# RWKV-7 mixer: operands laid out for both directions or both heads at once, score products in column halves

## Chip, cores and metric

One core of one Trainium2 chip runs the whole program. The metric is device time in microseconds (us), the median of three runs. Beside it there is one profiled execution, from which every row below comes.

## What is computed

The reference is a two-layer trunk over 1024 latent tokens and 256 context tokens (width 1024). A layer mixes tokens with three groups of heads (RWKV-7 in both directions, windowed attention, neighbourhood attention), all fed by one input projection, and then runs a hierarchical mixture of experts. The change is in the RWKV-7 group alone: 4 heads of 64, two directions, 1280 steps each of

```python
def _rwkv7_step(state, inp):
    r, w, k, v, kk, a = inp
    sk = jnp.einsum('dbhvk,dbhk->dbhv', state, kk)
    state = state * w[..., None, :] - sk[..., :, None] * (kk * a)[..., None, :] + v[..., :, None] * k[..., None, :]
    return state, jnp.einsum('dbhvk,dbhk->dbhv', state, r)
```

## The kernel before

`layer` runs per layer: layer norm and the part of the input projection that RWKV needs, then `rwkv`, then attention, output projection, routing, experts. While `rwkv` runs, the rest of the input projection (`in_A_rest`, `in_BC`; matmuls of L528 to L530 and L539 to L541) is issued piece by piece through `more()`, so that the two share TensorE.

`rwkv` works in chunks of 64 tokens. One **stage** `st` of ten takes 128 tokens (2 chunks, index `c`) of the forward direction and 128 of the backward one (`d`), for 4 heads as 2 pairs (`hp`) of 2 (`e`). Head `e` of a pair lives on partitions 0 to 63 or 64 to 127 (`hom[e]`). The parts of a stage:

- `front(st)` (L719 to L790), one stage ahead: decays by a scan along tokens (L746, one instruction per direction and head pair), exponentials, then the operands. `L1` holds kk times decay and r times decay: eight products of 64x256, four on VectorE (`e`=0) and four on GpSimd (`e`=1), L776 and L777. `bk` holds b and k (L784 on VectorE, L785 on GpSimd), `bw` (L788, GpSimd) is `bk` times the chunk's decay.
- Transposes of `bw` into `L2` (L809, copies L812).
- **Scores**: for each direction, eight products `pa` of [b|k] with [kk|r], 128x128 (L824), in two PSUM tiles. From each, VectorE masks the other head's half into `L1` (L829), a quarter into `Ly` (L831), and for `d`=1 another quarter into `low` (L833). For `d`=0 `low` has its own product `pf` (L840, L841). `pu`, `pb`, `pa` and `pf` share a ring of two PSUM buffers.
- **Inverse**: `low` goes to DRAM and comes back as lanes; `inv16` inverts the 16x16 diagonal blocks with 28 small VectorE instructions (L955, L956), and the result comes back through DRAM (L960, L963). Then `mm8` (L853) does three rounds of 16 products 64x64x64 (`pe4`, `pzt`, `pz`), each followed by a VectorE operation of 128x512 (L857, L858, L859), and L864 to L878 do the last 32x32 step.
- **State**: two steps per stage (`s`). Each is `px` (L904), a copy to `xy` (L906), `pu2` (L912), a negation split over ScalarE and VectorE (L913, L914), `pm` for the next state and the output (L924, L926), the new state (L930), and `ys`, the output, in four VectorE additions of 64x128 (L935). The value rows of the next state tile come by four ScalarE copies of 64x256 (`new_pvu`, L713). `ys` is stored once per stage (L940, two DMAs); `values` loads v with two DMAs (L705).

The code gives the order only in part: a scheduler in the framework orders each engine's queue by its own estimates of readiness, and every engine runs its queue strictly in that order. SyncE (SP) issues all these DMAs from one queue, and waits in it.

Of the kernel before, what the change touches and what calls it, by code (L numbers as in the profile page):

```python
# [9 lines left out]
F32 = mybir.dt.float32  # L10
# [12 lines left out]
P = 128  # L23
# [132 lines left out]
def _consts():  # L156
# [33 lines left out]
    for k in range(2):  # L190
        d[f"mL1_{k}"] = np.concatenate([np.concatenate([im[k], sm[k]], 1), np.concatenate([sm[k], im[k]], 1)], 0)
        d[f"mR_{k}"] = np.concatenate([im[k], im[k]], 0)
# [3 lines left out]
    d["mE4"] = np.concatenate([e4, e4], 0)  # L196
    d["scan"] = np.tile((np.arange(128) % 64 != 0).astype(np.float32), (128, 1))
# [106 lines left out]
class Trunk:  # L304
# [370 lines left out]
    def rwkv(self, l, rp, ps, tag, psc, tagc, psi, rest, more):  # L675
# [23 lines left out]

        vt = {}  # L700

        def values(st):
            vt[st] = rp.tile([P, 2, 2, 2, 64], F32, tag="vt", name="vt", bufs=2)
            for d, seg in enumerate((FSEG[st], BSEG[st])):
                nc.sync.dma_start(vt[st][:, d], self.vst[:, 2 * seg:2 * seg + 2])  # L705


        def new_pvu(st, s):
            t = rp.tile([P, 2, 2, 2, 2, 64], F32, tag="pvu", name="pvu", bufs=2)
            for d in range(2):  # L710
                for e in range(2):
                    o = hom[1 - e]
                    a.copy(t[o, d, :, :, e, :], vt[st][o, d, s if d == 0 else 1 - s].unsqueeze(1).to_broadcast([64, 2, 2, 64]))  # L713
            return t
# [4 lines left out]
        def front(st):  # L719
# [51 lines left out]
            L1v = L1.rearrange("p d c h e s t -> p d h e s c t")  # L771
            bku = bk.rearrange("p d h c s t -> p (d h c) s t")
            for d in range(2):
                for e in range(2):
# [6 lines left out]

            for e in range(2):
                o = hom[e]
                v.scalar_tensor_tensor(bku[o, :, e], units(b2)[o], 0.5, units(wv)[o], OP.mult, OP.mult)  # L784
                g.tensor_tensor(bku[o, :, 1 - e], units(kd)[o], units(wv)[o], OP.mult)  # L785

# [6 lines left out]
        for st in range(10):  # L793
# [16 lines left out]
            for e, pb in enumerate(pbs):  # L810
                for d in range(2):
                    a.copy(L2[:, d, :, :, e].rearrange("p c h t -> p h c t"), pb[:, 256 * d:256 * d + 256].rearrange("p (h c t) -> p h c t", h=2, c=2))  # L812

            def mask(m, p, n):
                return k2(m)[p].unsqueeze(1).unsqueeze(1).to_broadcast([p.stop - p.start, 2, 2, n])

            for d in range(2):

                pas = [ps.tile([P, 512], F32, tag=tag, name="pa") for _ in range(2)]
                for hp in range(2):  # L820
                    for c in range(2):
                        i = 2 * hp + c
                        for e in range(2):
                            te.matmul(pas[e][:, i * 128:i * 128 + 128], bk[hom[e], d, hp, c].rearrange("p s t -> p (s t)"),  # L824
                                      L1[hom[e], d, c, hp, e].rearrange("p s t -> p (s t)"), start=True, stop=True)
                for e, pa in enumerate(pas):
                    home, oth = hom[e], hom[1 - e]
                    pav = pa.rearrange("p (h c s t) -> p h c s t", h=2, c=2, s=2)
                    v.tensor_tensor(L1[oth, d, :, :, e].rearrange("p c h s t -> p h c (s t)"), pav[oth].rearrange("p h c s t -> p h c (s t)"),  # L829
                                    mask(f"mL1_{d}", oth, 128), OP.mult)  # L830
                    v.tensor_tensor(Ly[home, d].rearrange("p c h t -> p h c t"), pav[home, :, :, 1 - e], mask(f"mR_{d}", home, 64), OP.mult)  # L831
                    if d == 1:
                        v.tensor_tensor(low[home, 1], pav[home, :, :, e], mask("mLow", home, 64), OP.mult)  # L833

            pf = ps.tile([P, 512], F32, tag=tag, name="pf")
            for hp in range(2):
                for c in range(2):
                    for e in range(2):
                        i = 2 * hp + c
                        te.matmul(pf[hom[e], i * 64:i * 64 + 64], L1[hom[e], 0, c, hp, e, e, :], bk[hom[e], 0, hp, c, e, :], start=True, stop=True)  # L840
            v.tensor_tensor(low[:, 0], pf[:, 0:256].rearrange("p (h c t) -> p h c t", h=2, c=2), mask("mLow", slice(0, 128), 64), OP.mult)  # L841
# [6 lines left out]

            def mm8(name, lt, rh):
                o = psi.tile([P, 512], F32, tag="i", name=name)  # L850
                for u in range(8):
                    for e in range(2):
                        te.matmul(o[hom[e], u * 64:u * 64 + 64], lt[hom[e], u, :], rh[hom[e], u, :], start=True, stop=True)  # L853
                return o.rearrange("p (u t) -> p u t", t=64)
# [1259 lines left out]
```

## Time and profile before

| | us |
|---|---|
| median of three runs (3547.73 to 3562.64) | 3548.71 |
| profiled execution | 3544.36 |
| its span on the core | 3541.6 |
| `rwkv` of the first layer, about | 240 to 720 |
| `rwkv` of the second layer, about | 2000 to 2480 |

| engine | busy us | share of the span |
|---|---|---|
| TensorE matmul (PE) | 2930.6 | 83% |
| VectorE (DVE) | 2285.5 | 65% |
| ScalarE (ACT) | 1544.1 | 44% |
| GpSimd (POOL) | 1007.7 | 28% |

Shares are averages over stages with different limits, so only the two stretches of `rwkv` count here. Waits are shown by the instruction that waited and by the one that released it. The profile leaves digits off the ends of names: `L` is `L1` or `L2`, `pu` also `pu2`, `c` a table of constants, `z` the tiles `z16` of the inverse.

### The profile page before, as it was taken

What the parts mean: (1) busy time and instruction counts of PE and PEld (TensorE: products, weight loads), DVE (VectorE), ACT (ScalarE), POOL (GpSimd) and SP (SyncE); (2) the same over time, 40 slices, a digit from 0 to 9 for tenths busy, and PEclk for the clock granted to TensorE, in tenths of its full rate; (3) what the DMA queues carried; (4) which work ended last, traced back from release to release, by engine and by line L of the source; (5) the groups of instructions that cost most, each with busy time, mean ns of one, the idle gap of its engine ahead of it and who ended that gap; (6) DMA issues with size and microseconds to landing.
All of it is one profiled execution on the core that took longest, in us unless ns stands there. A gap on an engine that the chain in (4) does not pass through costs nothing. (4 is left out here: it accounts for less than half of the span.)

```text
span 3541.6 us, 71217 instructions
## 1 busy us (share of the span) xinstructions
PE 2930.6 (83%) x28620; PEld 1833.0 (52%) x28620; DVE 2285.5 (65%) x4614; ACT 1544.1 (44%) x2769; POOL 1007.7 (28%) x998
## 2 busy tenths in 40 slices
PE   7998889989998788888737998898889866778864
PEld 4656567666755444443325565666666443334431
DVE  4356877368769454557678677783776845554775
ACT  4342444345643154456544434443565314343651
POOL 1122453134424211111165225331433321101113
PEclk9998889999999899999858988899899978888987
DMA  9764343282355789999862542433732769899995
GB/s 375 297 194 111 80 104 89 70 237 71 113 176 199 278 315 384 385 379 367 334 227 78 158 106 77 105 103 95 200 107 73 258 235 363 338 393 364 349 347 198
DMA packets 425468, 773.11 MB, mean 218 GB/s; under 512 B 211152, under 2 KB 340848, under 8 KB 394160
## 3 DMA queue, kind: packets, MB, share of 16 engines
q1 hardware_dynamic: 388048, 697.84, 56.7%
q0 software_dynamic: 36368, 68.07, 5.7%
q8 instruction: 227, 3.72, 0.4%
q10 hardware_dynamic: 720, 2.62, 0.3%
q14 instruction: 105, 0.86, 0.1%
HBM read 653.31 MB, written 114.97 MB: 217 GB/s over the span
## 5 line engine op out<-in xcount | busy, mean ns | idle before, releaser
L1664 PE MATMUL pgate<-wgp,hT 128*32 128x256 f16 (+2 forms) x1704 | 353.1, 376 | 101.8 <-ACT wgp L1613 60.8
L1664 PEld LDWEIGHTS <-hT 128*32 128x32 f16 (+2 forms) x3408 | 206.7, 108 | 334.0 <-issue 172.7
L529 PE MATMUL acc<-hL,wH 128*128 128x256 f16 (+2 forms) x1040 | 346.4, 334 | 13.4 <-POOL hL L486 13.4
L528 PE MATMUL acc<-hH,wH 128*128 128x256 f16 (+2 forms) x1040 | 345.6, 335 | 7.6 <-DVE hH L485 6.6
L530 PE MATMUL acc<-hH,wL 128*128 128x256 f16 (+2 forms) x1040 | 345.4, 333 | 0.0
L1704 PE MATMUL pd<-wdp,gT 128*32 128x256 f16 (+2 forms) x1704 | 221.1, 369 | 37.6 <-DVE gT L1691 21.6
L1195 POOL TENSOR_SCALAR s<-s,rd 128x640 f32<-128x640 f32 (+2 forms) x216 | 171.6, 794 | 222.3 <-DVE rd L1191 97.4
L1622 POOL DMA_INDIRECT xg<-hmoe,map x69 | 87.7, 1271 | 508.4 <-PE ptx L1628 454.5
L1664 PE MATMUL pgate<-wup,hT 128*32 128x256 f16 (+1 forms) x1224 | 196.9, 347 | 19.8 <-DVE wup L1614 12.7
L1614 DVE SCALAR_TENSOR_TENSOR wgp<-wg,wgp 128x2048 f16<-128x2048 f32 x74 | 166.4, 2287 | 63.2 <-ACT wgp L1613 63.1
L1614 DVE SCALAR_TENSOR_TENSOR wdp<-wd,wdp 128x2048 f16<-128x2048 f32 x74 | 166.5, 2287 | 46.9 <-ACT wdp L1613 46.9
L1184 ACT ACTIVATE s<-s,nm 128x640 f32<-128x640 f32 (+2 forms) x216 | 164.4, 763 | 66.1 <-DVE nm L1181 48.6
L1614 DVE SCALAR_TENSOR_TENSOR wup<-wu,wup 128x2048 f16<-128x2048 f32 x74 | 166.3, 2286 | 30.0 <-ACT wup L1613 27.7
L1208 PE MATMUL po<-pt,vt 128*64 128x128 f32 x1920 | 166.9, 288 | 20.2 <-DVE pt L1199 11.7
L1293 PE MATMUL acco<-wo,o 128*128 128x512 f16 x756 | 177.2, 388 | 0.0
L1704 PEld LDWEIGHTS <-gT 128*32 128x32 f16 (+2 forms) x1704 | 97.0, 108 | 147.4 <-DVE gT L1691 30.0
L1613 ACT ACTIVATE wdp<-wd 128x2048 f16<-128x2048 f32 x74 | 137.2, 1903 | 51.0 <-DMA wd<-w_down 44.1
L1717 POOL DMA_DIRECT2D ys<-y x66 | 51.7, 784 | 378.5 <-DVE y L1711 206.9
L1613 ACT ACTIVATE wup<-wu 128x2048 f16<-128x2048 f32 x74 | 137.3, 1903 | 48.7 <-DMA wu<-w_up 48.7
L1613 ACT ACTIVATE wgp<-wg 128x2048 f16<-128x2048 f32 x74 | 137.4, 1902 | 46.0 <-DMA wg<-w_gate 42.7
L1165 PE MATMUL pss<-k,qs 128*128 128x256 f16 (+1 forms) x552 | 127.5, 269 | 31.9 <-DVE mx L1178 18.4
L1672 ACT ACTIVATE sg<-pgate 64x512 f32<-64x512 f32 (+2 forms) x86 | 42.8, 498 | 251.9 <-PE pgate L1664 251.9
(420 smaller groups left out, 7424.2 us busy)
## 6 DMA issues: line engine op xcount, KB each, us to landing
wu<-w_up SPq DMA_DIRECT2D x64, 2048.0 KB
wd<-w_down SPq DMA_DIRECT2D x64, 2048.0 KB
wg<-w_gate SPq DMA_DIRECT2D x64, 2048.0 KB
wmod<-w_mod SPq DMA_DIRECT2D x48, 1024.0 KB
w<-w_in SPq DMA_DIRECT2D x41, 512.0 KB
ld<-ys SPq DMA_DIRECT2D x40, 384.0 KB
z<-inv SPq DMA_DIRECT2D x80, 128.0 KB
ys<-y POOLq DMA_DIRECT2D x20, 512.0 KB
```

Of the source, the lines that this page charges most:

```text
L528: self.nc.tensor.matmul(ov, H[:, k, :], hh, start=k == 0, stop=False)
L529: self.nc.tensor.matmul(ov, H[:, k, :], hl, start=False, stop=False)
L530: self.nc.tensor.matmul(ov, Lo[:, k, :], hh, start=False, stop=k == KD - 1)
L1165: te.matmul(pss[:, o:o + n], qs[:, e, Q], k1[:, e, k0:k0 + n], start=True, stop=False)
L1184: a.activation(s2[:, e, :nk], s2[:, e, :nk], AF.Exp, bias=nm[:, e:e + 1], scale=1.0 / SS, accum_out=den[:, e:e + 1])
L1195: g.tensor_scalar(s2[:, e, :nk], s2[:, e, :nk], rd[:, e:e + 1], SC_Q, OP.mult, OP.mult)
L1208: te.matmul(po[64 * e:64 * e + 64, 0:P], vt[:, kb, 64 * e:64 * e + 64], pt[:, e, x * P:x * P + P], start=x == 0, stop=x == len(kbs) - 1)
L1293: te.matmul(acc, o[:, zo, k] if k < KD - 1 else self.og_last[:, zo, tok], wo[:, zw, k, c], start=k == 0 and y == 0, stop=k == KD - 1 and y ...
L1613: nc.scalar.mul(t[:, 0, c], w[:, c], SC_W)
L1614: nc.vector.scalar_tensor_tensor(t[:, 1, c], w[:, c], SC_W, t[:, 0, c], OP.mult, OP.subtract)
L1664: te.matmul(p[off + i * m:off + i * m + m, :n], part(hT, zh)[:, k, o:o + m], part(w, zw)[:, k, i * n:i * n + n], start=k == 0 and y == 0, ...
L1704: te.matmul(t, part(gT, zh)[:, k, :m], part(wd, zw)[:, k, i * n:i * n + n], start=k == 0 and y == 0, stop=k == 3 and y == len(parts) - 1)
```

## The change

Tiles change their axis order so that one instruction covers both directions or both heads. Per stage:

- Scans: 2 of 128x256 in place of 4 of 128x128.
- `L1`: 4 products of 64x512, all on VectorE and placed behind `bk`, in place of 4+4 of 64x256 on VectorE and GpSimd.
- Scores: `pa` gives way to `pk` (16 products, 64 rows and 64 output partitions by 128 columns, one PSUM tile per direction), `pr` (16 of 64x64) for `Ly` and `pf` (16 of 64x64, 8 before) for `low`. Masks: four of 64x512 as before, and one 128x512 each for `Ly` and `low` in place of four, two and one of 256 columns.
- `mm8` computes only the 32 columns of each 64 that are used. Its three VectorE operations have 128x256.
- `L2` copies 2 for 4, value copies 2 for 4 per step, `ys` 1 addition of 128x256 for 4 of 64x128 per step.
- `ys` is stored per step, two DMAs of 64 KB; `values` takes three DMAs for two.

```diff
-                for hp in range(2):
-                    v.tensor_tensor_scan(cum[:, d, hp], k2("scan"), th[:, d, hp], 0.0, OP.mult, OP.add)
+                v.tensor_tensor_scan(cum[:, d].rearrange("p h t -> p (h t)"), k2("scan"), th[:, d].rearrange("p h t -> p (h t)"), 0.0, OP.mult, OP.add)
...
-                    eng = v if e == 0 else g
-                    eng.tensor_tensor(L1v[hom[e], d, :, e, e], chv(kk_)[hom[e], d], chv(ex)[hom[e], d], OP.mult)
-                    eng.tensor_tensor(L1v[hom[e], d, :, e, 1 - e], chv(r_)[hom[e], d], chv(cum)[hom[e], d], OP.mult)
...
+                for i, (x, y) in enumerate(((kk_, ex), (r_, cum))):
+                    v.tensor_tensor(L1p[o, :, :, e, i], pieces(x)[o], pieces(y)[o], OP.mult)
...
             for d in range(2):
-                pas = [ps.tile([P, 512], F32, tag=tag, name="pa") for _ in range(2)]
...
+                pk = ps.tile([P, 4, 128], F32, tag=tag, name="pk")
                 for hp in range(2):
                     for c in range(2):
                         for e in range(2):
+                            te.matmul(pk[hom[1 - e], 2 * hp + c], bk[hom[e], d, hp, c, 1 - e, :],
+                                      L1[hom[e], d, hp, c, e].rearrange("p s t -> p (s t)"), start=True, stop=True)
+                for e in range(2):
+                    o = hom[1 - e]
+                    v.tensor_tensor(L1[o, d, :, :, e].rearrange("p h c s t -> p (h c) (s t)"), pk[o],
+                                    k2(f"mL1_{d}")[o].unsqueeze(1).to_broadcast([64, 4, 128]), OP.mult)
+            pr = ps.tile([P, 8, 64], F32, tag=tag, name="pr")
+            pf = ps.tile([P, 8, 64], F32, tag=tag, name="pf")
...
+                            te.matmul(pr[hom[e], i], b_, r1, start=True, stop=True)
+                            x, y = (K_, b_) if d == 0 else (b_, K_)
+                            te.matmul(pf[hom[e], i], x, y, start=True, stop=True)
+            v.tensor_tensor(Ly.rearrange("p d h c t -> p d (h c) t"), pr.rearrange("p (d u) t -> p d u t", d=2),
...
+            v.tensor_tensor(low.rearrange("p d h c t -> p (d h c) t"), pf, k2("mLow").unsqueeze(1).to_broadcast([P, 8, 64]), OP.mult)
...
+                o = psi.tile([P, 8, 2, 16], F32, tag="i", name=name)
...
+                        te.matmul(o[hom[e], u], lt[hom[e], u, :], rh[hom[e], u], start=True, stop=True)
...
+            v.tensor_tensor(Eh, mm8("pe4", lowu, up16), k2("mE4").rearrange("p (g t) -> p g t", t=16).unsqueeze(1).to_broadcast([P, 8, 2, 16]), OP.mult)
+            pzt = mm8("pzt", z16, Eh)
+            v.tensor_tensor(up16, up16, pzt, OP.subtract)
+            v.tensor_tensor(lo16, lo16, mm8("pz", E4, lo16), OP.subtract)
...
+                ys = rp.tile([P, 2, 2, 64], F32, tag="ys", name="ys", bufs=2)
+                v.tensor_tensor(ys, pm[:, 1], xy[:, 1], OP.add)
+                for d in range(2):
+                    nc.sync.dma_start(y_d[d, 2 * seg[d] + cs[d]], ys[:, d])
```

The scheduler's order moves with it. On VectorE, late in the second layer's `rwkv`, from the last masks of one stage to the products of the next `front`, before (`c` is the table of masks, `pvu` the state tile):

```order
L829 TENSOR_TENSOR L_25074<-pa,c_20752 64x2x2x128
L831 TENSOR_TENSOR Ly<-pa,c_20752 64x2x2x64
L833 TENSOR_TENSOR low<-pa,c_20752 64x256
L930 TENSOR_TENSOR pvu<-pmy,xw 64x2x2x64 x2
L935 TENSOR_TENSOR ys<-pmy,xy 64x128 x4
L857 TENSOR_TENSOR E<-pe_25339,c_20752 128x512
L754 TENSOR_TENSOR cum<-ex,th 128x256
L761 SCALAR_TENSOR_TENSOR th<-ta,ld 128x512
L841 TENSOR_TENSOR low<-pf,c_20752 128x256
L784 SCALAR_TENSOR_TENSOR bk<-th,wv 64x8x64 x2
L776 TENSOR_TENSOR L_25642<-ld,ex 64x2x2x64 x2
L777 TENSOR_TENSOR L_25642<-ld,cum 64x2x2x64 x2
```

The same place with the change:

```order
L790 TENSOR_TENSOR L_25691<-ld,ex 64x8x64
L790 TENSOR_TENSOR L_25691<-ld,cum 64x8x64
L828 TENSOR_TENSOR L_25120<-pk,c_20784 64x4x128 x4
L923 TENSOR_SCALAR pvu<-pu_24930 64x4x64
L866 TENSOR_TENSOR E_20794<-pe_25396,c_20784 128x16x16
L938 TENSOR_TENSOR pvu<-pmy,xw 64x4x64 x2
L940 TENSOR_TENSOR ys<-pmy,xy 128x256
L868 TENSOR_TENSOR z_1_25393<-z_1_25393,pzt 128x16x16
L869 TENSOR_TENSOR z_0_25389<-z_0_25389,pz 128x16x16
L842 TENSOR_TENSOR Ly<-pr,c_20784 128x512
L844 TENSOR_TENSOR low<-pf,c_20784 128x512
```

Four masks now follow each other; `Ly` and `low` come once each, behind the inverse's operations; the next `front`'s products stand ahead of the masks.

On TensorE at the same stage, around the last scores, before (`pmy` is `pm`, `pe` with 64x64 is `pe4`):

```order
L824 MATMUL pa<-L_25074,bk 128x128 x3
L926 MATMUL pmy<-pvu,L_24521 64x64
L824 MATMUL pa<-L_25074,bk 128x128
L926 MATMUL pmy<-pvu,L_24521 64x64 x7
L924 MATMUL pmy<-pvu,Ly 64x64 x8
L853 MATMUL pe_25339<-z_1_25335,low 64x64 x16
L840 MATMUL pf<-bk,L_25074 64x64 x5
L904 MATMUL px<-pvu,L_23975 64x64 x2
L840 MATMUL pf<-bk,L_25074 64x64 x2
L904 MATMUL px<-pvu,L_23975 64x64 x14
```

With the change:

```order
L861 MATMUL pe_25396<-z_1_25393,low 64x32 x3
L841 MATMUL pf<-bk,L_25120 64x64
L838 MATMUL pr<-L_25120,bk 64x64
L934 MATMUL pmy<-pvu,L_24560 64x64 x7
L932 MATMUL pmy<-pvu,Ly 64x64 x8
L841 MATMUL pf<-bk,L_25120 64x64
L838 MATMUL pr<-L_25120,bk 64x64
L841 MATMUL pf<-bk,L_25120 64x64
L861 MATMUL pzt<-E_20794,z_0_25389 64x32 x16
L838 MATMUL pr<-L_25120,bk 64x64
```

`pr` and `pf` alternate and stand strewn between the products of the inverse and of the state, where `pf` stood in two or three pieces. A `pmy` or a `pzt` behind a `pr` in this queue starts after it.

## Rows read from the trace of the kernel before

**Rows 1.** Busy time by engine; granted clock, DMA share, GB/s last: both stretches, one tail.
```profile
240.00:720.00 480.00, 425.00 (x5659) 301.67 (x5658) 327.48 (x760) 187.94 (x471) 175.53 (x171) 0.91 0.38 99
600.00:720.00 120.00, 115.89 (x1663) 82.81 (x1662) 52.98 (x148) 41.47 (x98) 21.41 (x26) 0.96 0.36 94
2000.00:2480.00 480.00, 421.33 (x5685) 298.69 (x5682) 336.91 (x779) 189.29 (x475) 180.01 (x169) 0.90 0.38 102
```

**Rows 2.** What TensorE waited for, 240 to 720: us in total, times, longest.
```profile
PE pe L864 <- DVE z L859: 7.0, 2, 5.4
PE pu L735 <- DVE low L841: 6.6, 3, 2.5
```

**Rows 3.** The same, 2000 to 2480.
```profile
PE pu L735 <- DVE low L841: 5.0, 2, 2.8
PE px L904 <- DVE L L829: 3.1, 1, 3.1
PE pz L853 <- DVE z L858: 2.9, 3, 2.3
```

**Rows 4.** The chain that ended last, by line, share of 2000 to 2480.
```profile
by line: PE acc L528 5.6%; PE acc L530 5.2%; PE acc L529 5.2%; issue 4.5%; PE pa L824 4.4%; DVE L L777 3.9%; PE px L904 3.4%; DVE il L955 3.2%; DVE L L776 2.9%; DVE bk L784 2.6%; PE pmy L926 2.6%; DVE zl L956 2.6%; PE accn L541 2.5%; PE acc
```

**Rows 5.** Two lines of VectorE: duration in ns, shortest, median, longest.
```profile
L784 DVE SCALAR_TENSOR_TENSOR bk<-th,wv x40: 672/1130/1751, 245.7 to 2367.1; 64x512 f32<-64x512 f32 x40
L776 DVE TENSOR_TENSOR L<-ld,ex x40: 406/941/1480, 242.7 to 2369.1; 64x256 f32<-64x256 f32 x40
```

**Rows 6.** VectorE groups that change: busy us in total, mean ns, idle before and releaser.
```profile
L829 DVE TENSOR_TENSOR L<-pa,c 64x512 f32<-64x512 f32 x80 | 54.8, 684 | 11.1 <-PE pa L824 10.2
L777 DVE TENSOR_TENSOR L<-ld,cum 64x256 f32<-64x256 f32 x40 | 42.5, 1095 | 0.2
L935 DVE TENSOR_TENSOR ys<-pmy,xy 64x128 f32<-64x128 f32 x160 | 39.0, 283 | 8.0 <-PE pmy L924 7.5
L776 DVE TENSOR_TENSOR L<-ld,ex 64x256 f32<-64x256 f32 x40 | 35.4, 918 | 0.7 <-ACT ex L757 0.5
L746 DVE TENSOR_TENSOR_SCAN cum<-c,th 128x128 f32<-128x128 f32 x80 | 34.9, 485 | 0.6
L831 DVE TENSOR_TENSOR Ly<-pa,c 64x256 f32<-64x256 f32 x80 | 33.8, 422 | 1.2
L833 DVE TENSOR_TENSOR low<-pa,c 64x256 f32<-64x256 f32 x40 | 16.6, 414 | 1.4 <-PE pe L864 1.3
L859 DVE TENSOR_TENSOR z<-z,pz 128x512 f32<-128x512 f32 x20 | 13.6, 678 | 4.7 <-PE pz L853 4.6
L841 DVE TENSOR_TENSOR low<-pf,c 128x256 f32<-128x256 f32 x20 | 8.4, 420 | 10.6 <-PE pf L840 10.2
```

**Rows 7.** TensorE groups that change, and one of 32 columns (two passes per product).
```profile
L824 PE MATMUL pa<-L,bk 64*128 64x128 f32 x640 | 80.5, 310 | 12.0 <-DVE zl L956 5.2 <-DVE Ly L831 4.2 <-ACT L L812 2.4
L853 PE MATMUL pe<-z,low 64*64 64x64 f32 x640 | 32.4, 243 | 22.5 <-DMA z<-inv 22.5
L853 PE MATMUL pz<-z,E 64*64 64x64 f32 x640 | 27.4, 235 | 3.6 <-DVE z L858 3.6
L853 PE MATMUL pzt<-E,z 64*64 64x64 f32 x640 | 25.0, 223 | 1.7 <-DVE E L857 1.7
L840 PE MATMUL pf<-bk,L 64*64 64x64 f32 x320 | 17.0, 235 | 2.8 <-DVE low L833 2.8
L864 PE MATMUL pe<-z,low 32*32 32x32 f32 x640 | 15.8, 200 | 8.9 <-DVE z L859 8.9
```

**Rows 8.** ScalarE copies: the value rows, and one of 512 columns.
```profile
L713 ACT COPY pvu<-vt 64x256 f32<-64x256 f32 x160 | 64.3, 403 | 129.3 <-PE pmy L924 119.1 <-DVE zl L956 4.4 <-DVE il L955 4.3
L906 ACT COPY xy<-px 128x512 f32<-128x512 f32 x40 | 23.3, 582 | 46.7 <-PE px L904 46.5
```

**Rows 9.** What SP's queue waited for, 2000 to 2480: us in total, times, longest.
```profile
SPq L844 <- DVE low L841: 37.4, 6, 11.1
SPq L940 <- DVE ys L935: 13.8, 3, 7.8
```

More of the change, by code (lines that the diff above doesn't have):

```diff
@@ L785, in front @@
                 g.tensor_tensor(bku[o, :, 1 - e], units(kd)[o], units(wv)[o], OP.mult)
+            L1p = L1.rearrange("p d h c e s t -> p d (h c) e s t")
+            for e in range(2):
+                o = hom[e]
+                for i, (x, y) in enumerate(((kk_, ex), (r_, cum))):
+                    v.tensor_tensor(L1p[o, :, :, e, i], pieces(x)[o], pieces(y)[o], OP.mult)
             bw = rp.tile([P, 2, 2, 2, 2, 64], F32, tag="bw", name="bw")
@@ L810, in rwkv @@
             for e, pb in enumerate(pbs):
[L811 to L815, printed above, removed]
+                a.copy(L2[:, :, :, :, e].rearrange("p d h c t -> p (d h c) t"), pb.rearrange("p (u t) -> p u t", t=64))
             for d in range(2):
-                pas = [ps.tile([P, 512], F32, tag=tag, name="pa") for _ in range(2)]
+                pk = ps.tile([P, 4, 128], F32, tag=tag, name="pk")
@@ L820, in rwkv @@
                 for hp in range(2):
                     for c in range(2):
-                        i = 2 * hp + c
                         for e in range(2):
[L824 to L841, printed above, removed]
+                            te.matmul(pk[hom[1 - e], 2 * hp + c], bk[hom[e], d, hp, c, 1 - e, :],
+                                      L1[hom[e], d, hp, c, e].rearrange("p s t -> p (s t)"), start=True, stop=True)
@@ L896, in rwkv @@
                         w = bass.AP(tensor=w.tensor, offset=w.offset + s, ap=[w.ap[0], [5 - 2 * s, 2], [2, 2], [0, 64]])
-                        g.tensor_tensor(xw[hom[e]], X[hom[e], :, 0, :, e, :], w, OP.mult)
+                        g.tensor_tensor(xw[hom[e]], X[hom[e], 0, :, :, e, :], w, OP.mult)
                 px = psc.tile([P, 2, 2, 2, 64], F32, tag=tagc, name="px")
-                for d in range(2):
-                    c = s if d == 0 else 1 - s
-                    for hp in range(2):
-                        for e in range(2):
-                            for sl in range(2):
-                                te.matmul(px[hom[sl], d, hp, e, :], L1[:, d, c, hp, e, sl, :], X[:, d, 0, hp, e, :], start=True, stop=True)
+                for sl in range(2):
+                    for d in range(2):
+                        for hp in range(2):
+                            for e in range(2):
+                                te.matmul(px[hom[e ^ sl], sl, d, hp, :], L1[:, d, hp, cs[d], e, sl, :], X[:, 0, d, hp, e, :], start=True, stop=True)
                 xy = rp.tile([P, 2, 2, 2, 64], F32, tag="xy", name="xy")
@@ L929, in rwkv @@
                     for e in range(2):
-                        v.tensor_tensor(nx[hom[e], :, 0, :, e, :], pm[hom[e], 0], xw[hom[e]], OP.add)
-                for e in range(2):
-                    o = hom[1 - e]
-                    for d in range(2):
-                        c = s if d == 0 else 1 - s
-                        v.tensor_tensor(ys[o, d, c], pm[o, 1, d], xy[o, d, :, e, :], OP.add)
+                        v.tensor_tensor(nx[hom[e], 0, :, :, e, :], pm[hom[e], 0], xw[hom[e]], OP.add)
+                ys = rp.tile([P, 2, 2, 64], F32, tag="ys", name="ys", bufs=2)
+                v.tensor_tensor(ys, pm[:, 1], xy[:, 1], OP.add)
+                for d in range(2):
+                    nc.sync.dma_start(y_d[d, 2 * seg[d] + cs[d]], ys[:, d])
                 if not last:
@@ L938, in rwkv @@
             more()
-            for d in range(2):
-                nc.sync.dma_start(y_d[d, 2 * seg[d]:2 * seg[d] + 2].rearrange("c p h t -> p c h t"), ys[:, d])
     def inv16(self, rp, b):
```

66 lines of the change are left out of this document (35 added, 31 removed).

## The prediction

> **What bounds the kernel now.** Busy time by engine over the two stretches of `rwkv` comes first, since nothing else changes [rows 1]. In each 480 us TensorE is busy 425 and 421 us, VectorE 327 and 337, GpSimd 176 and 180. TensorE is the fullest engine and yet idle for 55.0 and 58.7 us, 113.7 together; when VectorE's share of the work is over (600 to 720), TensorE fills 115.9 of 120 us and its granted clock averages 0.96 against 0.91 over the whole stretch. So these stretches are nearly TensorE-bound, with holes where its queue, which runs in order, meets a result that is not there. What opens the holes is in the waits [rows 2, 3]: some of them end with a VectorE operation which this change shortens or joins with others; the five largest of these hold 7.0 + 6.6 + 5.0 + 3.1 + 2.9 = 24.6 us. The chain of waits says how much of VectorE's work stands on the path [rows 4]: of the 480 us of the second stretch, L776 and L777 alone take 2.9% + 3.9%, or 32.6 us, of some 39 us that VectorE spends on them there (half of 35.4 + 42.5 [rows 6]): 84%.
>
> **VectorE, term by term** (20 stages in the two layers, totals from [rows 6]).
> - Scans: 34.9 us for 80 of 128 columns. Forty of 256 cost at most the same 34.9. From 256 to 512 columns a mask goes from 422 to 684 ns, a factor 1.62, and by that the scans would cost 34.9/80 x 1.62 x 40 = 28. I take 32: a scan costs more per column than a mask, so less of it is fixed.
> - Operands: 35.4 + 42.5 = 77.9 us now. Eighty products of 64x512 replace them. The nearest row is L784, of the same size, also two SBUF inputs, in the same place: 672 ns at best and 1130 at the median [rows 5]. That gives 54 to 90. I take 73, about the middle: GpSimd loses its four products per stage but still runs its half of `bk` and `bw` just then.
> - `Ly` and `low`: 33.8 + 16.6 + 8.4 = 58.8 us. Forty of 128x512 at 0.678 (L859's mean) are 27.
> - Inverse: three groups like L859, 40.8 us. Sixty of 128x256 at 0.42 (L841's mean) are 25.
> - Output: 39.0 us. Forty of 128x256 at 0.42 are 17.
> - The four masks stay (64x512, 684 ns).
>
> Sum: 251.4 to 174, **77 us less** (57 to 100).
>
> **The place where page and row differ, operands.** L776 takes 406 ns at best and 941 at the median [rows 5]; it reads two SBUF operands while GpSimd runs the other head's products. The Trainium skill, SBUF — State Buffer, section "SBUF: two separate sides", has VectorE and GpSimd take one shared port pair in turns, each for a whole instruction. The median agrees. By the page every new product that meets `bk` or `bw` on GpSimd would wait as L784 does, so the operands would stand at the upper end, 90 us, and the sum would lose 17 of its 77 us.
>
> **TensorE** [rows 7]. `pk` keeps the 128 columns of `pa` on half the output partitions: at most the same 80.5 us, at least two passes of 64 columns each, 2 x 27.4/640 x 640 = 55; I take 68. `pr` and `pf` make 1280 passes of 64 columns where 320 cost 17.0: at 43 ns (27.4/640) to 53 ns (17.0/320) 55 to 68; I take 60, 43 more. The three rounds of `mm8` cost 32.4 + 27.4 + 25.0 = 84.8. With 32 columns the nearest row is L864, 15.8 per 640, so 47 for three; the upper end is 85. I take 50, since 64 rows are loaded, 35 less. Net about -5 us (-25 to +51): **TensorE's own work does not shrink.**
>
> **ScalarE, GpSimd, DMA.** Value copies: 160 of 0.403 become 80 of at most 0.582 [rows 8], 18 us less, beside TensorE; ScalarE is under 40% busy there [rows 1], so I count nothing. GpSimd loses four products per stage and is under 40% busy as well: nothing. Three more DMA issues per stage and a store of `ys` in the middle of it lengthen SP's queue. SP already waits 13.8 us for `ys` in the second stretch [rows 9]; behind it can stand the store of `low`, which opens the inverse. I count nothing, because SP waits longer, 37.4 us, for `low` itself: it is mostly early. With that cover gone it would add up to as much again, 14 us a layer.
>
> **Sum.** A lower end: the five waits of 24.6 us shrink as their operations do (to about half, as 58.8 + 40.8 us go to 27 + 25): -12. An upper end: 84% of the 77 us is on the path: -65. I take **-25**, nearer the lower end, since TensorE fills 88% of the stretch and keeps its work: each hole that closes leaves TensorE as the bound. 3544.4 - 25 = 3519.4 on the scale of the profiled execution. That execution lies 4.3 us under the median of the runs, so I predict **3524 us**. A measurement of this kernel can tell about 0.5% (17.7 us) from no change.
>
> **Rivals.**
> 1. *The whole chain follows.* VectorE is what the path leans on, TensorE's holes close and its clock rises as in the tail: 3548.7 - 65 = 3484. For it: 84% of L776 and L777 on the path. Against: 65 of 113.7 us of holes would have to close, and only 24.6 of them show a changed releaser. 0.12.
> 2. *TensorE absorbs it.* The order keeps stalls where the inverse's round trip through DRAM and the state steps set the pace, and VectorE only idles more: 0 to -17 us, about 3540. For it: TensorE at 0.88 with unchanged work. 0.24.
> 3. *Narrow products cost as much as wide ones.* Then `mm8` stays at 85 us, TensorE gains 30 us of work instead of losing 5, and -25 + 30 gives 3554. Against: L864's passes of 32 columns take 25 ns, L853's of 64 columns 39 to 51 ns (shape differs too). 0.05. The Trainium skill, TensorEngine Tiling (Array Packing), section "Instruction Overhead", puts some 60 cycles under every matmul, so that one column costs what sixty do; it speaks for this rival, the rows against it.
> 4. *The ring of two PSUM buffers: slower.* `pr` needs the buffer of the first `pk`, `pf` that of the second. Both therefore wait for all four masks, 4 x 0.684 = 2.7 us in VectorE's queue, and they stand strewn among `pmy`, `pzt` and `px`, which then wait too. Uncovered, 20 x 2.7 = 55 us, and -25 + 55 gives 3579. It decides from 1.25 us per stage upward (no gain left), and gives a measurable loss from 2.1 us. For it: the ring already makes `pu` wait for `low` (6.6 + 5.0 us [rows 2, 3]). Against: most stages have input-projection matmuls between `pk` and `pr`. 0.17.
>
> **Chances and range.** The forecast's own case has 0.42. Faster by over 0.5%: 0.42 + 0.12 = 0.54; within: 0.24 + 0.05 = 0.29; slower: 0.17. The range runs from 3486, where half of rival 1 is left out, to 3562, where a good half of rival 4 is (0.06 and 0.10). The forecast's own case spans 3510 to 3531.
>
> **What would show it.** In the changed profile VectorE's busy time should fall by some 77 us (2285 to about 2208) and GpSimd's by about as much, if its half of the operands costs what VectorE's does (77.9). TensorE's should stay within 25 us or so, with `mm8` near 50 us in three groups, `pk` near 68. The four operand products should average about 0.9 us. Idle TensorE in the two stretches should fall from 113.7 to about 90, and the second layer's stretch should begin some 12 us earlier. The forecast is wrong if `pr` or `pf` waits over 25 us in all for a mask (rival 4), if the `mm8` groups stay above 75 us (rival 3), or if VectorE's time falls as computed and TensorE's idle time does not (rival 2).

## The result: slower, and by another step than the one feared

The changed kernel takes **3581.85 us** (median of 10 runs) against 3547.35 us before (10 runs): ratio **1.0091** (95% interval 1.0073 to 1.0109), some 34 us more. The prediction of 3524 us and its range up to 3562 both lie under it. Below, a kernel's ratio is always that to the kernel before, measured on the same chip, with the 95% interval in brackets; the kernel before had medians of 3547 to 3556 us there, so ratios compare better than times.

The profile after, busy time by engine (page, part 1):

```profile
PE 2946.5 (82%) x29580; PEld 1853.2 (52%) x29580; DVE 2227.6 (62%) x4354; ACT 1523.0 (43%) x2649; POOL 943.8 (26%) x920
```

VectorE did lose work (2285.5 to 2227.6 us), and so did GpSimd (1007.7 to 943.8). The two stretches, as in [rows 1] (columns: length; busy us and count of PE, PEld, DVE, ACT, POOL; granted clock; DMA share; GB/s):

```profile
240.00:720.00 480.00, 411.21 (x6006) 300.07 (x6005) 296.65 (x622) 171.74 (x397) 142.01 (x126) 0.88 0.36 91
2000.00:2480.00 480.00, 416.64 (x5797) 294.57 (x5792) 304.35 (x626) 173.30 (x395) 142.91 (x124) 0.88 0.38 99
```

TensorE is idle 68.8 + 63.4 = 132.2 us of them where it was idle 113.7, at a mean granted clock of 0.88 (a mix of its two levels, 1.2 GHz or 0.5 and 2.4 GHz or 1) where it was 0.91 and 0.90. So VectorE's saving didn't reach TensorE, which waits 18.5 us more. Over the whole span TensorE is idle for 627.0 us (611.0 before) and busy for 2946.5 (2930.6): of the 31.9 us by which the profiled span grew, half is idle time and half is matmul time. How long `rwkv` now lasts is told by the copies to `xy`, one per state step (operation; min/median/max ns; first and last start), second layer only, after and then before:

```profile
L916 ACT COPY xy<-px x20: 558/585/589, 2065.0 to 2503.3; 128x512 f32<-128x512 f32 x20
```

```profile
L906 ACT COPY xy<-px x20: 561/585/587, 2051.6 to 2454.9; 128x512 f32<-128x512 f32 x20
```

The second layer's first copy comes 13.4 us later and the last 48.4 us later. In the first layer the last copy is 19.1 us later (710.3 against 691.2). Of the 48.4 us some 16 are made up behind the stretch, and 31.9 are left in the span (3573.5 against 3541.6).

Where the waiting is: whole-trace waits of TensorE, then of VectorE (engine, line and what it waited for: us in total, times, longest), first after, then before:

```profile
PE pe L861 <- DMA z<-inv: 50.1, 18, 12.5
...
PE pmy L934 <- DVE pvu L923: 34.0, 17, 3.5
...
DVE zl L955 <- DMA al<-lan: 88.6, 17, 7.2
```

```profile
PE pe L853 <- DMA z<-inv: 22.5, 15, 3.9
PE pmy L926 <- DVE pvu L914: 21.9, 7, 9.4
...
DVE zl L950 <- DMA al<-lan: 26.5, 12, 5.3
```

These are TensorE's waits for the inverse's result (`pe4`) and for the negated state (`pvu`), and VectorE's for the inverse's lanes (`al`). They have grown by 27.6, 12.1 and 62.1 us. Of the waits that the prediction counted on, the two of `pu` for `low` (6.6 + 5.0 us [rows 2, 3]) are gone, and those for the inverse's operations stay (7.5 us at L874). What grew was not in the sum.

The groups that answer to [rows 6] and [rows 7] (line, engine, tiles, shapes, count; busy us, mean ns; idle before):

```profile
L790 DVE TENSOR_TENSOR L<-ld,cum 64x512 f32<-64x512 f32 x40 | 64.7, 1619 | 0.3
...
L790 DVE TENSOR_TENSOR L<-ld,ex 64x512 f32<-64x512 f32 x40 | 48.5, 1213 | 0.6
...
L749 DVE TENSOR_TENSOR_SCAN cum<-c,th 128x256 f32<-128x256 f32 x40 | 26.4, 698 | 0.3
...
L940 DVE TENSOR_TENSOR ys<-pmy,xy 128x256 f32<-128x256 f32 x40 | 17.0, 425 | 8.1 <-PE pmy L932 6.9
...
L842 DVE TENSOR_TENSOR Ly<-pr,c 128x512 f32<-128x512 f32 x20 | 13.8, 689 | 28.8 <-PE pr L838 25.4 <-PE pf L841 3.4
L844 DVE TENSOR_TENSOR low<-pf,c 128x512 f32<-128x512 f32 x20 | 13.6, 682 | 0.1
```

```profile
L824 PE MATMUL pk<-L,bk 64*64 64x128 f32 x640 | 53.4, 314 | 3.8 <-ACT L L816 3.8
L838 PE MATMUL pr<-L,bk 64*64 64x64 f32 x640 | 48.9, 256 | 13.3 <-DVE L L828 7.7 <-DVE zl L961 5.4
...
L861 PE MATMUL pe<-z,low 64*64 64x32 f32 x640 | 37.4, 254 | 50.2 <-DMA z<-inv 50.1
...
L861 PE MATMUL pzt<-E,z 64*64 64x32 f32 x640 | 28.6, 242 | 0.3 <-DVE E L866 0.3
L841 PE MATMUL pf<-L,bk 64*64 64x64 f32 x320 | 27.8, 254 | 0.0
L861 PE MATMUL pz<-z,E 64*64 64x32 f32 x640 | 25.7, 234 | 2.4 <-DVE z L868 2.4
L841 PE MATMUL pf<-bk,L 64*64 64x64 f32 x320 | 24.3, 258 | 4.7 <-DVE L L828 4.1 <-DVE zl L961 0.4
```

Three terms are far from the forecast: the operands (113.2 us instead of 73), `pr` and `pf` (101.0 instead of 60), and `mm8` (91.7 instead of 50). Each is a suspect, and so are the later `low` and the stores of `y` between the steps.

### The profile page after: what moved, and what is told of

It reads as the page before. It is cut to its first block, busy times and chain, and to the rows that moved or that the text cites. A ratio compares the mean times of both kernels' runs of the same rounds, so it can differ in the third digit from the quotient of the medians.

```text
span 3573.5 us, 72683 instructions
## 1 busy us (share of the span) xinstructions
PE 2946.5 (82%) x29580; PEld 1853.2 (52%) x29580; DVE 2227.6 (62%) x4354; ACT 1523.0 (43%) x2649; POOL 943.8 (26%) x920
## 5 line engine op out<-in xcount | busy, mean ns | idle before, releaser
L1618 ACT ACTIVATE wgp<-wg 128x2048 f16<-128x2048 f32 x74 | 137.4, 1903 | 53.4 <-DMA wg<-w_gate 48.3
L530 PEld LDWEIGHTS <-wL 128*128 128x128 f16 (+1 forms) x1040 | 104.7, 101 | 83.3 <-issue 26.6
```

Source lines behind the costliest of these rows:

```text
L530: self.nc.tensor.matmul(ov, Lo[:, k, :], hh, start=False, stop=k == KD - 1)
L1618: nc.scalar.mul(t[:, 0, c], w[:, c], SC_W)
```

## Experiments

Four suspects were undone one at a time, each in the changed kernel. Each of these four kernels also gets an order of its own, so a run here clears its suspect only within what an order is worth (about 1%, as the later runs show).

**e1_l1_split**: the operands of `e`=1 back to GpSimd.

```diff
-                    v.tensor_tensor(L1p[o, :, :, e, i], pieces(x)[o], pieces(y)[o], OP.mult)
+                    (v, g)[e].tensor_tensor(L1p[o, :, :, e, i], pieces(x)[o], pieces(y)[o], OP.mult)
```

> The changed kernel with one part taken back: the two operand products of e=1 go to GpSimd again (64x512 each), VectorE keeps the two of e=0. If the operands on VectorE beside GpSimd's products are what costs (113.2 us on VectorE in the changed kernel against 77.9 before), VectorE's share falls to 40 to 55 us, GpSimd gains 45 to 65, and the time comes back by 15 to 34 us, to 3548 to 3567. If the loss lies in the scores, or in the way the queues are ordered around the inverse, the time stays within 10 us of the changed kernel's 3582, though VectorE still loses its 60 us.

3602.14 us, ratio 1.0158 (1.0129 to 1.0187). VectorE's operands fell to 55.7 us (33.2 + 22.5), and the kernel got some 20 us slower. Nothing here says that the operands on VectorE cost the time.

**e2_old_scores**: `pa` and the one-direction `pf` in place of `pk`, `pr` and `pf`.

```diff
-                pk = ps.tile([P, 4, 128], F32, tag=tag, name="pk")
+                pas = [ps.tile([P, 512], F32, tag=tag, name="pa") for _ in range(2)]
...
```

> The changed kernel with its score products taken back to 128x128 ones (pa, and pf for the forward direction alone) and the masks of before, in the new layout. TensorE's part should fall from 53.4 + 48.9 + 52.1 = 154.4 us (pk, pr, pf) to about 80.5 + 17.0 = 97.5, so 57 us less; VectorE's masks for Ly and low rise from 27.4 to about 59. If the extra passes of pr and pf, and the late low behind them, are what costs, the time falls by 25 to 45 us, to 3537 to 3557. If VectorE's operands are the cause, the added 31 us on VectorE make it no faster: 3575 to 3595.

3579.48 us, 1.0084 (1.0059 to 1.0108): no change, though `pa` and `pf` took 85.5 + 17.3 us for 154.4. So the passes of `pr` and `pf` don't show as the cost either.

**e3_full_columns**: the three rounds of `mm8` and their VectorE operations at full width.

```diff
-            v.tensor_tensor(Eh, mm8("pe4", lowu, up16), k2("mE4")...to_broadcast([P, 8, 2, 16]), OP.mult)
+            v.tensor_tensor(E, mm8("pe4", lowu, zt16), k2("mE4").unsqueeze(1).to_broadcast([P, 8, 64]), OP.mult)
...
```

> The changed kernel with the three rounds of mm8 back at 64 columns and their three VectorE operations at 128x512. If a 64-row product costs the same at 32 and at 64 columns, the three groups stay at 85 to 95 us on TensorE (91.7 now), VectorE gains about 16 us, and the time moves by less than 10 us from 3582. If the halves do save passes that the records hide, TensorE's groups rise by 30 us or more and the time by 15 to 30 us.

**3520.78 us, 0.9926 (0.9901 to 0.9950)**: faster than both kernels, by the edit of which least was expected, and within 4 us of the forecast for the whole change. Neither theory foresaw it: the products cost 32.3 + 26.8 + 24.2 = 83.3 us at full width, so the halves had saved nothing there that could be given back.

**e4_y_per_stage**: `y` stored once per stage.

```diff
-                for d in range(2):
-                    nc.sync.dma_start(y_d[d, 2 * seg[d] + cs[d]], ys[:, d])
+            nc.sync.dma_start(y_d[0, 2 * seg[0]:2 * seg[0] + 2].rearrange("c p h t -> p c h t"), ys[:, :, 0])
+            for s in range(2):
+                nc.sync.dma_start(y_d[1, 2 * seg[1] + 1 - s], ys[:, s, 1])
...
```

> The changed kernel with the output stored once per stage, behind both steps (three DMAs in place of four, none between the steps). SyncE waits some 68 us in the second layer's stretch before stores of y, most of it behind operations that the inverse waits for. If these waits hold up low, al and the inverse's transfers, the time falls by 15 to 30 us, to 3552 to 3567, and TensorE's wait of 50.1 us for the inverse's first result falls below 35. If the queue is early anyway, the time stays within 8 us of 3582.

3577.64 us, 1.0084 (1.0061 to 1.0106). The wait for the inverse's first result did halve (24.7 us), and the time stayed: that wait alone isn't the loss, and taking the extra stores out of SyncE's queue gains nothing. The wait for the negated state grew meanwhile, from 34.0 to 48.8 us.

**What do the halves cost?** Three things changed with them: the products' columns, VectorE's operations, and the order, which the scheduler makes anew when sizes change.

**e5_wide_products**: products at 64 columns, VectorE on halves.

```diff
-                        te.matmul(o[hom[e], u], lt[hom[e], u, :], rh[hom[e], u], start=True, stop=True)
+                        te.matmul(o[hom[e], u], lt[hom[e], u, :], rh[hom[e], u, :], start=True, stop=True)
...
```

> The changed kernel with the three rounds of mm8 at 64 columns again, while VectorE's three operations stay on the halves (128x256). Putting both back gave 3521 us, so one of three things costs 61 us: the narrow products themselves, VectorE's operations on halves, or only the order that the scheduler makes when it is told shorter durations. Narrow products as the cause: 3510 to 3535. VectorE's operations on halves as the cause: 3570 to 3590. The order alone: anything between 3510 and 3600, and the groups on TensorE and VectorE then cost what they did in the changed kernel (about 25 to 37 us a round, 425 ns an operation), while TensorE's wait for the inverse's result moves with the time.

3552.34 us, 0.9994 (0.9979 to 1.0008): about half of the way. That is outside what was expected of the products alone and of VectorE's operations alone. The order alone would fit, but so it would any time in a wide range; the wait for the inverse's first result moved with the time, to 36.5 us.

**e6_before_halves**: the halves alone, put into the kernel before.

```diff
-            v.tensor_tensor(zt16, zt16, mm8("pzt", z16, E), OP.subtract)
-            v.tensor_tensor(z16, z16, mm8("pz", E, z16), OP.subtract)
+            v.tensor_tensor(up16, up16, pzt, OP.subtract)
+            v.tensor_tensor(lo16, lo16, mm8("pz", E4, lo16), OP.subtract)
...
```

> The kernel before with the mm8 halves alone (products of 32 columns and VectorE operations on halves). If the halves cost time in themselves, 3580 to 3610. If a 64-row product costs the same at both widths and the rest is the order, VectorE saves 16 us, TensorE nothing, and the time is within 20 us of 3552 on either side, with no rise above 3575.

3568.56 us, 1.0048 (1.0031 to 1.0065): VectorE does 31 us less (2254.1 against 2285.5), and the kernel loses 0.5%.

**e7_pr_then_pf** and **e8_low_first**: the changed kernel's own instructions, written in another order. e7 (the diff) has all 16 of `pr` ahead of all 16 of `pf`; e8 has `pf` and `low` ahead of `pk`, and `pr` and `Ly` behind it.

```diff
             pr = ps.tile([P, 8, 64], F32, tag=tag, name="pr")
-            pf = ps.tile([P, 8, 64], F32, tag=tag, name="pf")
...
                             te.matmul(pr[hom[e], i], b_, r1, start=True, stop=True)
+            pf = ps.tile([P, 8, 64], F32, tag=tag, name="pf")
+            for d in range(2):
...
                             te.matmul(pf[hom[e], i], x, y, start=True, stop=True)
```

> The changed kernel with the 16 pr products written ahead of the 16 pf products rather than one by one in turns. No instruction differs in kind, size or number. If the time is set by the work and by the waits that it makes, it stays within 8 us of 3582. If the order that the scheduler makes decides, it moves by 10 us or more either way.

> The changed kernel with pf and low written ahead of pk and its masks, and pr and Ly behind them. The same instructions in another order: low needs no masked operand, so it can start the inverse's way through DRAM some 3 to 6 us earlier in each stage. If the late low is what opens the waits around the inverse (TensorE 50.1 us for its first result, VectorE 88.6 us for the lanes), these fall by half and the time by 25 to 50 us, to 3532 to 3557. If the inverse's way is not on the path, the time stays within 10 us of 3582.

3583.24 us, 1.0082 (1.0062 to 1.0101), and 3585.03 us, 1.0091 (1.0070 to 1.0112). Both stay. In e8 the wait for the inverse's first result halves as expected (25.1 us), that for the lanes falls less (73.3), and again nothing is gained.

**A square of widths and orders.** To part the widths from the order, the program is built twice. The first build gives only the order of every engine's queue. In the second, each instruction gets a pure order edge (no semaphore) behind its forerunner in that queue:

```diff
+                        if last is not None and seen[n][1] == seen[last][1]:
+                            tc.add_manual_dep(seen[n][0], last, mybir.DependencyInfo(mybir.DependencyClass.NoSync, ...), reason="order")
...
+    for i in build(ORDER_OF).all_instructions():
+        order.setdefault(str(i.engine), []).append(i.name)
+    nc = build(SHAPE, order)
```

The changed kernel itself is the fourth corner (halves, in the order made for halves). It differs from e10 in one detail besides the order: its products write a packed PSUM tile, those of e10 the halves of a full one. In the traces VectorE, ScalarE and GpSimd run the same instructions in the same sequence in e11 as in the changed kernel, and in e10 as in e9.

> The base of a square of orders and widths, from one source: the three rounds of mm8 at 64 columns with VectorE operations of 128x512, on the zeroed tile of the changed kernel, in the order that the scheduler makes of that. It is the kernel of e3 up to the tile that holds the masked product, and a little of its order. If e3's gain belongs to the whole widths, 3510 to 3535. If it was luck of one order, anything up to 3590.

> The halves of the changed kernel (products of 32 columns, VectorE operations of 128x256), with every engine's queue held to the order that the scheduler made for the whole widths (that of e9), instruction by instruction. If the order is what the halves lose by, this runs like e9 or up to 16 us faster, since VectorE's operations are shorter: 3500 to 3535. If the halves cost time on the chip (in the products, or through TensorE's clock), it loses most of the 61 us again: 3560 to 3585.

> The whole widths (64 columns, 128x512), with every queue held to the order that the scheduler made for the halves, which is the changed kernel's own. If the order decides, this stays at the changed kernel's 3582 or goes up to 16 us over it for VectorE's longer operations: 3575 to 3600. If the halves cost time on the chip, it comes down to 3520 to 3545.

| | order made for the whole widths | order made for the halves |
|---|---|---|
| whole widths | e9: 3532.22, 0.9934 (0.9908 to 0.9959) | e11: 3573.05, 1.0056 (1.0037 to 1.0075) |
| halves | e10: 3533.78, 0.9946 (0.9928 to 0.9964) | changed kernel: 3581.85, 1.0091 (1.0073 to 1.0109) |

**The order carries the loss**: 1.2% between the columns at whole widths, 1.5% at halves. Between the rows there is 0.1% and 0.4%, and it doesn't favour the halves. TensorE's clock is no rival at whole widths: the median over all runs of its mean granted clock is 0.896 in e9 and 0.895 in e11. At the halves it falls along with the order, from 0.8935 in e10 to 0.8855 in the changed kernel.

The trace shows the order at work in single stalls. The eighth `pe4` of the first layer in the changed kernel, in e11 and in e10 (start, us, engine, line; in brackets the idle time before it):

```profile
580.81 0.23 PE L539 MATMUL accn<-wH,hH 128*128 128x128 f16 x1
593.52 0.39 PE L861 MATMUL pe<-z,low 64*64 64x32 f32 x2 [12.47 <-DMA z<-inv]
593.84 0.29 PE L540 MATMUL accn<-wH,hL 128*128 128x128 f16 x1
```

```profile
588.16 0.45 PE L863 MATMUL pe<-z,low 64*64 64x64 f32 x2 [12.60 <-DMA z<-inv]
```

```profile
607.64 0.30 PE L865 MATMUL pe<-z,low 64*64 64x32 f32 x2 [0.38 <-DMA z<-inv]
```

The changed kernel and e11 differ in every width of `mm8` and share this hole of 12.5 us; e10 has the halves and not the hole. Over the whole trace the waits of e11, of e10 and of e9:

```profile
PE pe L863 <- DMA z<-inv: 47.0, 21, 12.6
PE pmy L939 <- DVE pvu L928: 41.3, 19, 3.9
...
DVE zl L960 <- DMA al<-lan: 89.4, 17, 7.1
```

```profile
PE pe L865 <- DMA z<-inv: 20.0, 15, 4.0
PE pmy L939 <- DVE pvu L928: 16.6, 9, 3.4
...
DVE zl L960 <- DMA al<-lan: 63.6, 12, 10.2
```

```profile
PE pe L863 <- DMA z<-inv: 23.9, 13, 4.1
PE pmy L939 <- DVE pvu L928: 15.2, 10, 3.9
...
DVE zl L960 <- DMA al<-lan: 64.6, 13, 8.3
```

Those of e11 are near the changed kernel's (50.1, 34.0, 88.6), those of e10 near e9's. What the order does at that hole stands in VectorE's timeline, from `low` on (start, us), first in the changed kernel, then in e10:

```profile
570.55 0.68 DVE L844 TENSOR_TENSOR low<-pf,c 128x512 f32<-128x512 f32 x1
...
579.84 0.42 DVE L955 TENSOR_TENSOR zl<-c,al 64x256 f32<-64x256 f32 x1 [7.09 <-DMA al<-lan]
...
586.64 0.37 DVE L962 COPY zl<-zl 64x256 f32<-64x256 f32 x1
586.93 0.41 DVE L746 TENSOR_SCALAR th<-th 128x512 f32<-128x512 f32 x1
```

```profile
570.78 0.68 DVE L844 TENSOR_TENSOR low<-pf,c 128x512 f32<-128x512 f32 x1
577.64 0.42 DVE L960 TENSOR_TENSOR zl<-c,al 64x256 f32<-64x256 f32 x1 [6.18 <-DMA al<-lan]
577.98 0.41 DVE L746 TENSOR_SCALAR th<-th 128x512 f32<-128x512 f32 x1
578.31 0.16 DVE L965 TENSOR_TENSOR il<-al,zl 64x14 f32<-64x14 f32 x1
578.42 1.27 DVE L749 TENSOR_TENSOR_SCAN cum<-c,th 128x256 f32<-128x256 f32 x2
```

In the changed kernel VectorE stands 7.09 us at `zl` for the lanes, runs the inverse as one block (579.84 to 587.01), and begins the next `front` only behind it. TensorE's queue has `pe4` ahead of the input projection's next products (`accn`), so they wait through the hole as well: one starts at 580.81, the next at 593.84. In e10 VectorE waits nearly as long for the lanes (6.18 us), but the next `front` is woven between the inverse's small steps, and TensorE has its products and more of `accn` ahead of `pe4`.

The idle time isn't the whole price. Behind the hole the clock is at its lower level. The changed kernel's stretches after it (columns as in the result; 593.5 to 600 and 600 to 607 us):

```profile
593.50:600.00 6.50, 6.48 (x85) 5.55 (x87) 1.60 (x4) 1.34 (x3) 1.22 (x2) 0.50 0.08 23
600.00:607.00 7.00, 7.00 (x139) 6.44 (x139) 6.47 (x9) 4.34 (x11) 2.89 (x2) 0.91 0.09 24
```

In e10 the granted clock is 1.00 from 575 to 612 us. Over the whole span the changed kernel's TensorE is busy 53.0 us longer than e10's on the same products (2946.5 against 2893.5, at mean clocks of 0.885 and 0.900 in these two profiles) and idle only 3.0 us longer. At whole widths it is the other way round: e11 is idle 27.2 us longer than e9 and busy 14.6 us longer. How much of this is the clock's doing alone was not tested.

The three rounds of `mm8` in e9 (64 columns) and e10 (32 columns), the same order:

```profile
L863 PE MATMUL pe<-z,low 64*64 64x64 f32 x640 | 31.0, 238 | 24.1 <-DMA z<-inv 23.9
L863 PE MATMUL pzt<-E,z 64*64 64x64 f32 x640 | 26.8, 234 | 7.4 <-DVE E L872 7.4
L863 PE MATMUL pz<-z,E 64*64 64x64 f32 x640 | 24.4, 225 | 0.0
```

```profile
L865 PE MATMUL pe<-z,low 64*64 64x32 f32 x640 | 30.6, 236 | 22.8 <-DMA z<-inv 20.0 <-DVE bk L784 2.8
L865 PE MATMUL pzt<-E,z 64*64 64x32 f32 x640 | 27.3, 235 | 9.0 <-DVE E L872 9.0
L865 PE MATMUL pz<-z,E 64*64 64x32 f32 x640 | 24.2, 225 | 0.0
```

82.2 and 82.1 us: **half the columns, the same time.** The ends of matmuls are modelled in this profile, but their starts agree: in unbroken rows of `pz` at a granted clock of 1, one record starts 29.6 ns after the one before it on average in e9 and 28.8 in e10.

**Is it a kind or a chance?** e12 and e16 to e18 put the edits of e2, e1, e7 and e8 on e3, so that each has a partner with whole widths. e13 to e15 hold the queues to orders made for sizes that the kernel itself doesn't have: e13 (whole widths) and e14 (the kernel before) to one made for 128 columns in `mm8`, e15 (halves) to one made for 32 columns and whole VectorE operations. The product of which e13's and e14's orders are made:

```diff
+                        if self.wide == 2:
+                            n = min(u, 6)
+                            te.matmul(o[hom[e], n:n + 2], lt[hom[e], u, :], rh[hom[e], n:n + 2, :], start=True, stop=True)
```

> The kernel of e3 (whole widths in mm8) with the score products of before as well. TensorE should lose about 55 us of passes (154 to 98) and VectorE gain 31. In e2 this moved nothing, with the halves in place. If the passes of pr and pf weigh on the path once the inverse is in time, 3490 to 3510. If VectorE's masks or the order weigh as much, within 12 us of 3521.

> The whole widths (e9's program), with every queue held to the order that the scheduler makes for a program in which each product of mm8 has 128 columns; that program itself doesn't run. If the order is bad because the plan counts the inverse's steps too short, telling it longer ones moves other work in front of them: TensorE's wait for the inverse's first result (23.9 us in e9, 50.1 in the changed kernel) falls below 20 and the time is 3505 to 3532. If the halves' order was a chance and any other is as good or bad, the time lies anywhere between 3520 and 3590 and the wait with it.

> The kernel before, instruction for instruction, with every queue held to the order that the scheduler makes if each product of mm8 has 128 columns. The halves alone, which tell the plan shorter steps, cost this kernel 13 us (e6). If short steps in the plan are what costs, longer ones give something back: 3525 to 3548, with the wait for the inverse's first result under its 22.5 us. If it is chance, 3545 to 3590.

> The halves, with every queue held to the order that the scheduler makes for products of 32 columns but VectorE operations of 128x512. Products told wide and operations told short gave 3552 (e5), both told short 3582, both told long 3532 to 3534. If each estimate that is too short adds its part, 3545 to 3565 here. If the products alone matter (the chip takes as long for 32 columns as for 64, while it does take less for the shorter operations), 3570 to 3585.

> The kernel of e3 with the operand products of e=1 on GpSimd, as in e1, in the order that the scheduler makes of it. VectorE's operands fall from 103 us to 45 to 55, GpSimd gains 50 or so. If the operands on VectorE cost time once the inverse is in time, 3490 to 3510. If GpSimd's longer turn is later than VectorE's (e1 was 20 us slower than the changed kernel), 3525 to 3560.

> The kernel of e3 (whole widths in mm8) with the pr products written ahead of the pf products, as in e7 (3583 with the halves). If plans made for the halves are worse as a kind, this one lies under 3562, as the whole widths did in e3, e9, e12, e13 and e16 (3521 to 3559). If e3 was the chance of one order, it lies anywhere up to 3590.

> The kernel of e3 (whole widths in mm8) with pf and low written ahead of pk, as in e8 (3585 with the halves). If plans made for the halves are worse as a kind, under 3562. If chance, anywhere up to 3590.

| edit on the changed kernel | halves | whole widths |
|---|---|---|
| none | 3581.85, 1.0091 | e3: 3520.78, 0.9926 |
| operands of `e`=1 on GpSimd | e1: 3602.14, 1.0158 | e16: 3534.25, 0.9954 (0.9938 to 0.9970) |
| old scores | e2: 3579.48, 1.0084 | e12: 3559.46, 1.0016 (0.9996 to 1.0037) |
| `pr`, then `pf` | e7: 3583.24, 1.0082 | e17: 3554.27, 1.0010 (0.9994 to 1.0026) |
| `low` first | e8: 3585.03, 1.0091 | e18: 3552.94, 1.0000 (0.9985 to 1.0016) |

Five pairs of five fall the same way, by 0.7% to 2.0%, and the square gives the widths themselves 0.4% at most: this speaks for orders made for the halves being worse as a kind in this program. (The first pair raised the question, and in every pair widths and order change together.) But "tell the scheduler longer steps" is no remedy. e13 came to 3543.12 us, 0.9976 (0.9962 to 0.9989), worse than e9 and outside the 3505 to 3532 us expected of such a remedy; its wait for the inverse's first result was 26.1 us, not under 20. e14 came to 3598.43 us, 1.0129 (1.0105 to 1.0153): the kernel before, instruction for instruction, 46 us slower by its order alone, slower than either expectation allowed, and with a *shorter* wait for the inverse's first result (13.2 us against 22.5). e15 came to 3580.68 us, 1.0086 (1.0064 to 1.0108): telling it 32 columns for the products suffices, with whole VectorE operations in the plan.

That fits one reading: an order is best when planned with the durations that the chip has. As e9 and e10 show, the chip takes as long for 32 columns as for 64, so a plan that takes the halves as shorter is off, and so is one made for 128. **This reading is argued, not shown**: the profile doesn't hold the scheduler's own estimates, and that single orders are good or bad by chance stays a rival. Nor does one wait carry the loss in every bad order: the wait for the inverse is 50.1 us in the changed kernel and 24.7 in e4, at the same time.

## Why the prediction was wrong

- **The step that failed is the sum.** It took "five waits of 24.6 us halve" and "84% of 77 us is on the path" from the trace of the kernel before, so it took the order as given. The front part of this text shows that the order moves, and no term was set against that. One of the five waits was also misread: the 3.1 us of `px` end with a mask that the change leaves as it was (64x512, 684 ns). What the runs show in place of the saving is the cost of the order made for the halves: against e9 TensorE waits 26.2 us more at `pe4` and 18.8 more at `pmy`, and VectorE 24.0 more for the lanes (the other 38.1 of the 62.1 stand in e9 too, which is faster than the kernel before). By the square that order is worth 1.2% to 1.5%, some 41 to 48 us, more than the loss.
- **`mm8`, "I take 50"**: 91.7 us, and 82.1 in the better order, equal to 64 columns there. The nearest row, L864, was the wrong one: its products differ in rows as well as columns, and e10 shows that columns alone save nothing. So rival 3's mechanism is true (I gave it 0.05), while its price, 30 us, came from the products and not from the order that they bring. The Trainium skill, TensorEngine Tiling (Array Packing), section "Instruction Overhead", has one column cost what sixty do; by that, as an estimate, 32 columns save next to nothing against 64, and e9 and e10 agree (82.2 and 82.1 us). I had set that rule behind a row that did not test it.
- **Operands, 73 us (54 to 90)**: 113.2, above the upper end. The source view of L790 has 674 ns at best, as hoped, but 1593 and 1668 at the median:

```profile
L790 DVE TENSOR_TENSOR L<-ld,ex x40: 674/1593/1694, 244.3 to 2393.2; 64x512 f32<-64x512 f32 x40
L790 DVE TENSOR_TENSOR L<-ld,cum x40: 675/1668/2375, 245.7 to 2394.8; 64x512 f32<-64x512 f32 x40
```

  Most of them run while GpSimd makes `kd` or its half of `bk`, whose source view gives a median of 1611 ns. The Trainium skill, SBUF — State Buffer, section "SBUF: two separate sides", lets one of the two hold the shared ports for its whole instruction; the medians agree with turns taken one by one. The upper end borrowed from L784 (1130 ns) was too low: in the trace before, 27 of its 40 executions lay mostly beside GpSimd's operand products of 64x256 (medians 1108 and 1127 ns there), and 10 beside `kd` (median 1666), and the change takes the short products away. It cost no visible time: with half of the products back on GpSimd, e1 is slower than the changed kernel and e16 no faster than e3.
- **`pr` and `pf`, 60 us (55 to 68)**: 101.0. Again no time is seen to hang on it: e2 removes the excess and moves nothing, and e12 is 0.9% slower than e3.
- **Right**: `Ly` and `low` 27.4 (27), output 17.0 (17), `pu` no longer waiting for `low`. Better than foreseen, just below the lower bounds: scans 26.4 (32 taken, 28 the bound), `pk` 53.4 (68, bound 55). VectorE's busy time fell by 58 us (77 foreseen).
- **Rival 4** ended near the measured time (3579), by another road: the waits of `pr` and `pf` for masks are 7.7 + 4.1 us, not 55. It should not be called right.
- **Rival 2** named the place, "the inverse's round trip through DRAM and the state steps", but took the order there for no worse than before.
- With the halves taken back, the forecast's number comes out: e3 at 3521 and e9 at 3532. The other parts are then worth up to -0.74%, but e17 and e18, the same work in other orders, are at 1.0010 and 1.0000. So even that agreement holds only to within the 1% that an order is worth; that e3 came within 4 us is luck.

## What to carry to other kernels

Where a scheduler orders the queues from estimated sizes, every edit of a size is also an edit of the order, and here the order was worth up to 1.3% (46 us) with not one instruction changed (e14), more than the 25 us that the whole sum came to. Before crediting or blaming an edit, hold the queues to one order and change the sizes, then do the reverse; a square of four runs tells the two apart. And a narrower product is a saving only if a row of that very shape shows it: if it isn't one, the plan may still believe in it.

The version to keep is e3: all of the change but the halves, 3520.78 us, 0.9926 of before. Part of its gain is its own order, since e17 and e18 have the same work and none of it.

## What the runs showed of the hardware that was not expected

- Narrow products went with a lower granted clock at the order made for the halves: the mean over the whole span is 0.883 to 0.888 in the ten runs of the changed kernel and 0.893 to 0.897 in the nine of e11. At the other order it is less clear: 0.890 to 0.900 in e10, 0.894 to 0.904 in e9 (in the two stretches of their profiles 0.90 and 0.91 against 0.92 twice). This may be why VectorE's shorter operations (in e10 20 us less busy time than in e9) bought nothing, but it wasn't tested by itself.
- Written by turns, `pr` and `pf` took 101.0 us in the records. Written one behind the other they took 79.4 in e7 (first `pr`, then the two groups of `pf`):

```profile
L835 PE MATMUL pr<-L,bk 64*64 64x64 f32 x640 | 36.7, 262 | 21.3 <-DVE zl L963 9.7 <-DVE L L828 6.0 <-DVE il L962 5.6
L843 PE MATMUL pf<-bk,L 64*64 64x64 f32 x320 | 22.1, 269 | 0.5 <-DVE L L828 0.3 <-DVE il L962 0.2
L843 PE MATMUL pf<-L,bk 64*64 64x64 f32 x320 | 20.6, 259 | 0.0
```

  With whole widths it was 101.3 by turns (e3) and 70.5 in sequence (e17). Neither pair got faster by it; why the turns cost more was not looked into.
